# Down projections of two feed-forward layers by seven block products instead of eight

## The chip, the cores and the metric

The kernel runs on one core of a Trainium2 chip. Times are device microseconds, for one launch of the whole kernel. Five engines with instruction queues of their own work beside each other: TensorE (PE; the load of its stationary operand is listed as PEld), VectorE (DVE), ScalarE (ACT), GpSimd (POOL) and SyncE (SP), which issues the DMAs. Each works its queue strictly in order, so an instruction that waits holds up all that stand behind it there.

## The reference

One decoder layer over 512 tokens of width 1024, all in float32. Each feed-forward layer is a SwiGLU with 2816 inner columns, added at half weight:

```
x = x + 0.5 * swiglu(rms_norm(x, ffn1_norm), w_gate, w_up, w_down)
...        # attention and RWKV-7 mixing, projected in by w_in and out by w_out, added to x
x = x + 0.5 * swiglu(rms_norm(x, ffn2_norm), w_gate, w_up, w_down)

def swiglu(h, w_gate, w_up, w_down):
    return (jax.nn.silu(h @ w_gate) * (h @ w_up)) @ w_down
```

The down projection is the last product: 512 x 2816 by 2816 x 1024.

## The kernel before

A float32 product is made of three matmuls on rounded parts (`mm3`, lines 71 to 77): each operand is split into a high part, by a cast on ScalarE, and a rest, by a subtraction on VectorE, and high x high, high x rest and rest x high are summed in PSUM. Weights come in tiles of 512 KB. `weights` (lines 62 to 70) issues the load into one of three raw buffers (`raw_...`, line 64), casts it (`hi_...`, line 68) and subtracts (`lo_...`, line 69); of each of the two results there are two buffers.

*Gate and up* (`ffn`) take 22 blocks `f` of 128 inner columns. For each, two weight tiles (gate, up) meet the transposed input (`xa` in layer 1, `xc` in layer 2) in 2 x 8 x 3 matmuls of 128x512; SiLU (line 197) and a product (line 198) give `sg`, 128 inner columns by 512 tokens, which is split into `hh` and `hl` (lines 205, 206), the stationary operands of down. For the first block, the token columns come in two halves, and the norms and transposes of the last two token tiles are called in between (`proj_into` with `hook`).

*Down* (`rows_out`, lines 149 to 185) takes the 1024 output columns in two halves. In each, 11 groups of two blocks (one weight tile a group) are multiplied into four PSUM accumulators, one for each tile of 128 tokens. The last four groups are held back and finished tile by tile, so that a tile's addition into x (line 173), its norm (`norm_T`) and its transposes run under the next tile's matmuls. What comes after the last tile is handed to the next product as `hook`.

The order of instructions on an engine is that of the program as a list scheduler has merged it; it follows data, buffers and a few fixed pairs (`keep_in_program_order`). A tile that is allocated waits until the last user of its buffer is done.

Of the kernel before, what the change touches and what calls it, by code (L numbers as in the profile page):

```python
# [42 lines left out]
def tile_layer(ctx: ExitStack, tc: tile.TileContext, I, out):  # L43
# [99 lines left out]
    def rows_out(wsrc, n_grp, lhs, resid, scale, ptile, extra, done, name, dump=None, store=None, begun=None):  # L143
# [41 lines left out]

    def ffn(n, xT, x, hpool, ptile, extra, hook, done, w0, store):
        hT = []
# [31 lines left out]
    with ExitStack() as c:  # L219
        xpool = c.enter_context(tc.tile_pool(name="x1", bufs=1, reuse_waits="tile"))  # L220
        hpool = c.enter_context(tc.tile_pool(name="h1", bufs=1, reuse_waits="tile"))
        extra = c.enter_context(tc.tile_pool(name="e1", bufs=2, reuse_waits="tile"))
# [55 lines left out]
    with ExitStack() as c:  # L278
        xpool = c.enter_context(tc.tile_pool(name="x2", bufs=1, reuse_waits="tile"))
        xcpool = c.enter_context(tc.tile_pool(name="xc", bufs=4, reuse_waits="tile"))  # L280
        hpool = c.enter_context(tc.tile_pool(name="h2", bufs=1, reuse_waits="tile"))
# [776 lines left out]
```

## Time and profile before

| | us |
|---|---|
| median of 3 runs | 1140.79 |
| lowest, highest of the runs | 1138.6, 1566.35 |
| profiled execution, its own time | 1137.05 |
| its span, first to last instruction | 1135.3 |
| TensorE busy, share of the span | 1103.2, 97% |
| VectorE, ScalarE, GpSimd busy | 494.4, 383.9, 139.2 |
| DMA, mean over the span | 111.88 MB, 99 GB/s |

All numbers of the profile are of one execution, whose span lies between its first and last instruction. The first layer's gate and up run from about 18 to 257 us, its down to 379, mixing to about 770, the second layer's gate and up to about 1011 and its down to 1131. Matmuls are pipelined, so the duration of one contains a part of the next; the distance of their starts tells the pace.

### The profile page before, as it was taken

The page shows a single profiled execution, that of the slowest core. Times are in us where ns is not written, and L with a number is a line of the kernel's source. Part 1 is how long each engine was busy: PE and PEld are TensorE (multiplying, and loading weights), DVE is VectorE, ACT ScalarE, POOL GpSimd, SP SyncE. Part 2 cuts the span into 40 slices and gives each one's busy share as a digit, 9 for nine tenths or more (in the row PEclk, how much of TensorE's full clock was granted, in tenths as well). Part 3 has the DMA queues.
Part 4 walks back from the last instruction along what each step waited for, and adds up shares of the span by engine and source line. Part 5 has one row for each costly group of instructions (what it writes and reads, how often), then busy time and mean ns, then how long its engine had stood idle before and what let it go on. Part 6 is the DMA issues. An engine that isn't in the chain of part 4 may idle for free.

```text
span 1135.3 us, 13758 instructions
## 1 busy us (share of the span) xinstructions
PE 1103.2 (97%) x5512; PEld 921.3 (81%) x5512; DVE 494.4 (44%) x815; ACT 383.9 (34%) x604; POOL 139.2 (12%) x185
## 2 busy tenths in 40 slices
PE   7999999999999999998899999999999999999998
PEld 6888888888888977777788898779888888888887
DVE  5333333332223545695478467644333333332222
ACT  4322233222222356524343534433322232222120
POOL 3000000000000346302432211212000000000000
PEclk9999999999999999998899999999999999999999
DMA  5322332223224424542321200422223322233321
GB/s 189 111 93 96 105 97 93 93 100 105 93 93 148 163 69 102 150 130 83 94 63 60 90 23 29 148 75 94 93 93 103 101 93 93 95 105 104 122 94 56
DMA packets 53202, 111.88 MB, mean 99 GB/s; under 512 B 20721, under 2 KB 26097, under 8 KB 53138
## 3 DMA queue, kind: packets, MB, share of 16 engines
q1 hardware_dynamic: 53138, 111.00, 30.2%
q8 instruction: 43, 0.70, 0.3%
q14 instruction: 21, 0.17, 0.0%
HBM read 100.50 MB, written 9.44 MB: 97 GB/s over the span
## 4 chain that ended last, share of the span: by engine, by line
PE 85%; DVE 7%; ACT 3%; POOL 2%; issue 2%; DMA 1%; SPq 0%; POOLq 0%; ACTq 0%; DVEq 0%
PE gu L77 14%; PE gu L73 14%; PE gu L76 14%; PE accd L76 7%; PE accd L73 7%; PE accd L77 7%; PE in L77 3%; PE in L76 3%; PE in L73 3%; PE aa L844 1%; PE cx L870 1%; PE po L768 1%; PE cn L887 1%; DVE pr L642 1%; PE acco L76 1%
## 5 line engine op out<-in xcount | busy, mean ns | idle before, releaser
L68 ACT CAST hi_gu<-raw_gu 128x1024 fp32r<-128x1024 f32 x88 | 92.7, 1054 | 316.9 <-PE gu L76 299.6
L69 DVE TENSOR_TENSOR lo_gu<-raw_gu,hi_gu 128x1024 fp32r<-128x1024 f32 x84 | 102.9, 1225 | 158.5 <-ACT hi_gu L68 154.6
L76 PE MATMUL accd<-lo_d,hh 128*128 128x512 f32 x288 | 112.3, 390 | 0.0
L77 PE MATMUL accd<-hi_d,hl 128*128 128x512 f32 x288 | 112.1, 389 | 0.0
L73 PE MATMUL accd<-hi_d,hh 128*128 128x512 f32 x288 | 112.0, 390 | 0.0
L69 DVE TENSOR_TENSOR lo_d<-raw_d,hi_d 128x1024 fp32r<-128x1024 f32 x44 | 53.3, 1224 | 127.4 <-ACT hi_d L68 127.0
L68 ACT CAST hi_d<-raw_d 128x1024 fp32r<-128x1024 f32 x44 | 45.6, 1052 | 152.7 <-PE accd L77 133.0
L198 DVE TENSOR_TENSOR sg<-gu,sg 128x512 f32<-128x512 f32 x44 | 30.4, 692 | 143.2 <-PE gu L77 141.8
L76 PE MATMUL gu<-xa0l,hi_gu 128*128 128x512 f32 (+1 forms) x184 | 70.0, 380 | 0.5 <-DVE xa0l L130 0.5
L73 PE MATMUL gu<-xa0h,hi_gu 128*128 128x512 f32 (+1 forms) x184 | 70.1, 381 | 0.3 <-ACT xa0h L129 0.3
L73 PE MATMUL gu<-xc0h,hi_gu 128*128 128x512 f32 (+1 forms) x184 | 70.0, 380 | 0.0
L73 PE MATMUL gu<-xc1h,hi_gu 128*128 128x512 f32 (+1 forms) x184 | 70.0, 380 | 0.0
L73 PE MATMUL gu<-xa1h,hi_gu 128*128 128x512 f32 (+1 forms) x184 | 70.0, 380 | 0.0
L76 PE MATMUL gu<-xc0l,hi_gu 128*128 128x512 f32 (+1 forms) x184 | 69.9, 380 | 0.0
L77 PE MATMUL gu<-xc0h,lo_gu 128*128 128x512 f32 (+1 forms) x184 | 69.9, 380 | 0.0
L76 PE MATMUL gu<-xa1l,hi_gu 128*128 128x512 f32 (+1 forms) x184 | 69.9, 380 | 0.0
L76 PE MATMUL gu<-xc1l,hi_gu 128*128 128x512 f32 (+1 forms) x184 | 69.9, 380 | 0.0
L77 PE MATMUL gu<-xc1h,lo_gu 128*128 128x512 f32 (+1 forms) x184 | 69.9, 380 | 0.0
L77 PE MATMUL gu<-xa0h,lo_gu 128*128 128x512 f32 (+1 forms) x184 | 69.9, 380 | 0.0
L77 PE MATMUL gu<-xa1h,lo_gu 128*128 128x512 f32 (+1 forms) x184 | 69.9, 380 | 0.0
L76 PEld LDWEIGHTS accd<-lo_d,hh 128*128 128x128 f32 x288 | 54.1, 188 | 11.6 <-DVE lo_d L69 0.5
L73 PEld LDWEIGHTS accd<-hi_d,hh 128*128 128x128 f32 x288 | 53.9, 188 | 11.5 <-ACT hi_d L68 0.4
(349 smaller groups left out, 2253.4 us busy)
## 6 DMA issues: line engine op xcount, KB each, us to landing
raw_gu<-in_ffn_w_gu SPq DMA_DIRECT2D x88, 512.0 KB, 3.4
raw_d<-in_ffn_w_down SPq DMA_DIRECT2D x44, 512.0 KB, 3.4
raw_in<-in_w_in SPq DMA_DIRECT2D x28, 512.0 KB, 3.9
raw_o<-in_w_out SPq DMA_DIRECT2D x8, 512.0 KB, 3.4
x<-in_x SPq DMA_DIRECT2D x4, 512.0 KB, 5.8
xd<-x SPq DMA_DIRECT2D x4, 512.0 KB, 2.6
xr<-ard SPq DMA_DIRECT2D x8, 256.0 KB, 4.5
bk<-bkd SPq DMA_DIRECT2D x4, 512.0 KB, 4.3
```

The source lines that it names most:

```text
L68: A.copy(out=hi, in_=raw)
L69: (lo_eng or V).tensor_tensor(out=lo, in0=raw, in1=hi.bitcast(F32), op=ALU.subtract)
L73: first = T.matmul(ps, lh, rh, start=start, stop=False)
L76: T.matmul(ps, lh, rl, start=False, stop=False)
L77: T.matmul(ps, ll, rh, start=False, stop=stop)
L198: V.tensor_tensor(out=sg, in0=ps[1], in1=sg, op=ALU.mult)
L642: V.tensor_tensor(out=pr[:, :n1, :n2], in0=au[:, i + 1:, i:i + 1].broadcast_to([P, n1, n2]), in1=tu[:, i:i + 1, :n2].broadcast_to([P, n1, ...
L768: T.matmul(po[:, h, 0:65], pw[:, j * P:(j + 1) * P], va[:, j, h, 0:65], start=(j == 0), stop=(j == qi))
L844: T.matmul(ps[:, c], bk[:, j, c], xr[:, j, c, 2 * h:2 * h + 2], start=True, stop=True)
L870: T.matmul(px[:, j, h], xr[:, j, c, 2 * h:2 * h + 2].rearrange("p a b -> p (a b)"), sv[:, j, h, c, :], start=True, stop=True)
L887: T.matmul(pn[:, j, h], kr[:, j, c, 2 * h:2 * h + 2].rearrange("p a b -> p (a b)"), sv[:, j, h, c, :], start=True, stop=True)
```

## The change

Strassen's scheme multiplies 2x2 blocks with seven products instead of eight. The blocks are here: for activations, token half (tiles 0, 1 and 2, 3) by even or odd block `f` of a pair; for weights, even or odd `f` by column half. Four of the seven products take a sum of weight blocks and one more takes two weights' sums: five sums (128x512 each) for each of the 11 pairs. `sums_ahead` loads both halves of a pair's weights during gate and up, makes the sums on VectorE, and stores them in DRAM (`sd`: three, `s17`: two). `combine` makes the sums of activations from two `sg`. `down` then runs three stages of 11 groups: products 3 and 5, products 1 and 7, products 4, 2 and 6, whose last three groups are held back. Each product has two accumulators, for the two tiles of a token half, and is added into one or two places of x by `add`. Between stages, `split` turns the activation buffers into the next stage's sums. The down projection of mixing (`w_out`) still uses `rows_out`.

A layer's down issues 66 weight loads where it had 22: in the first stage and in the third, a tile comes as two loads of 256 KB.

```diff
-    def ffn(n, xT, x, hpool, ptile, extra, hook, done, w0, store):
-        hT = []
...
+    def sums_ahead(n):
+        wd = I[f'ffn{n}_w_down']
+        sd = dpool.tile([NG, 3, P, S], F32, name=f"sd{n}")
+        s17 = dpool.tile([NG, P, D], F32, name=f"s17{n}")
+        def steps():
+            t = ra = rb = None
+            for g in range(NG + 1):
+                if g:
+                    for o, i in ((sd[g - 1, 0:2].rearrange("j p s -> p j s"), t), (sd[g - 1, 2], rb[:, 0]), (s17[g - 1], ra)):
+                        tc.keep_in_program_order(Q.dma_start(out=o, in_=i.rearrange("p a b -> p (a b)") if i is ra else i))
+                if g == NG:
+                    return
+                ra, rb = (npool.tile([P, 2, S], F32, tag="xn", name=f"r{k}{n}_{g}") for k in "ab")
+                for k, z in enumerate((ra, rb)):
+                    tc.keep_in_program_order(Q.dma_start(out=z.rearrange("p a b -> p (a b)"), in_=wd[k, g]))
+                yield
+                t = npool.tile([P, 2, S], F32, tag="gain", bufs=1, name=f"s{n}_{g}")
+                V.tensor_tensor(out=t[:, 0], in0=rb[:, 0], in1=rb[:, 1], op=ALU.subtract)
+                V.tensor_tensor(out=t[:, 1], in0=ra[:, 1], in1=ra[:, 0], op=ALU.subtract)
+                V.tensor_tensor(out=rb[:, 0], in0=rb[:, 0], in1=ra[:, 0], op=ALU.add)
+                for j in range(2):
+                    V.tensor_tensor(out=ra[:, j], in0=ra[:, j], in1=rb[:, 1], op=ALU.add)
+                yield
+        return sd, s17, steps()
+    def combine(n, g, e, o, u, v, l):
+        V.tensor_tensor(out=u[0][:, 0], in0=e[:, 0:H], in1=o[:, H:S], op=ALU.add)
+        V.tensor_tensor(out=u[0][:, 1], in0=o[:, 0:H], in1=o[:, H:S], op=ALU.subtract)
+        V.tensor_tensor(out=u[1][:, 0], in0=e[:, H:S], in1=o[:, H:S], op=ALU.add)
+        V.tensor_tensor(out=u[2], in0=e[:, H:S], in1=e[:, 0:H], op=ALU.subtract)
+        A.copy(out=u[1][:, 1], in_=o[:, H:S])
+        split(v[:, 0], l[:, 0], e[:, 0:H])
+        V.tensor_tensor(out=o[:, 0:H], in0=e[:, 0:H], in1=o[:, 0:H], op=ALU.add)
...
+    def split(hi, lo, src):
+        A.copy(out=hi, in_=src)
+        V.tensor_tensor(out=lo, in0=src, in1=hi.bitcast(F32), op=ALU.subtract)
+    def down(n, U, VV, LL, x, ptile, xp, extra, sd, s17, done, dump, store):
+        wd = I[f'ffn{n}_w_down']
+        cnt = [0]
+        def loaded(name, *src, keep=None, to=None):
+            raw = wpool.tile([P, 2, S], F32, tag="wraw", bufs=3, name=f"raw_{name}")
...
+                for j, z in enumerate(src):
+                    Q.dma_start(out=raw[:, j], in_=z)
+            if to:
+                hi, lo = to
+                for j in range(len(hi)):
+                    A.copy(out=hi[j], in_=raw[:, j])
+                    V.tensor_tensor(out=lo[j], in0=raw[:, j], in1=hi[j].bitcast(F32), op=ALU.subtract)
+                return
+            cnt[0] += 1
...
+            A.copy(out=hi, in_=raw)
+            V.tensor_tensor(out=lo, in0=raw, in1=hi.bitcast(F32), op=ALU.subtract)
+            return hi, lo
...
+        def prod(acc, g, hl, w, ts=(0, 1), last=NG - 1):
+            for t in ts:
+                lh, ll = (z[:, t * P:(t + 1) * P] for z in hl)
+                mm3(acc[t], lh, ll, w[0], w[1], g == 0, g == last)
...
+        def add(acc, t, r, c, sign):
+            tt = 2 * r + t
+            xs = x[tt][:, c * S:(c + 1) * S]
+            V.scalar_tensor_tensor(out=xs, in0=acc[t], scalar=0.5 * sign, in1=xs, op0=ALU.mult, op1=ALU.add)
+            if (tt, c) in final and store:
...
+        def both(ma, mb, g, v, l, hi, lo):
+            pend.append((g, v, l, hi, lo))
+            if g != NG - 2:
+                for j, m in enumerate((ma, mb)):
+                    for g_, v, l, hi, lo in pend:
+                        prod(m, g_, (v[:, j], l[:, j]), (hi[:, j], lo[:, j]))
+                pend.clear()
...
+        for g in range(NG):
+            v, l = VV[g], LL[g]
+            hi, lo = loaded(f"d1{n}_{g}", sd[g, 0], wd[1, g][:, S:D])
+            both(m3, m5, g, v, l, hi, lo)
+            for k in (g - 1, g) if g == NG - 1 else (g,) if g != NG - 2 else ():
+                split(VV[k], LL[k], U[k][0])
+        for t in range(2):
+            add(m3, t, 0, 1, 1)
+            add(m3, t, 1, 1, 1)
+        for t in range(2):
+            final.add((t, 1))
+            add(m5, t, 0, 1, 1)
+            add(m5, t, 0, 0, -1)
+        ms = [None] * NT
...
+        def turn(g):
+            split(VV[g], LL[g], U[g][1])
+            if g == 0:
...
+                x6.append(VV[g - 4])
+            split(x6[g][:, 0], x6[g][:, 1], U[g][2])
+        m1, m7 = accs(1), accs(7, "tp")
+        for g in range(NG):
+            v, l = VV[g], LL[g]
+            hi, lo = loaded(f"d2{n}_{g}", s17[g])
+            both(m1, m7, g, v, l, hi, lo)
+            if g >= NG - 3:
+                turn(g - NG + 3)
...
+        m4, m2, m6 = accs(4), accs(2), accs(6)
+        keep = 3
+        held, w6 = [], {}
+        for g in range(NG):
+            v, l = VV[g], LL[g]
+            kept = g >= NG - keep
+            hi, lo = loaded(f"d3{n}_{g}", wd[0, g][:, 0:S], sd[g, 1],
...
+            if g % 2 == 0:
+                gs = [k for k in (g, g + 1) if k < NG]
+                if g < NG - keep:
+                    h6, l6 = loaded(f"d6{n}_{g}", *(sd[k, 2] for k in gs))
...
+                else:
+                    for k in gs:
+                        w6[k] = tuple(LL[2 * (k - NG + keep) + p].rearrange("p a b -> p (a b)") for p in range(2))
+                    loaded(f"d6{n}_{g}", *(sd[k, 2] for k in gs), to=([w6[k][0] for k in gs], [w6[k][1] for k in gs]))
+            z = ((v[:, 1], l[:, 1]), (hi[:, 1], lo[:, 1])), ((v[:, 0], l[:, 0]), (hi[:, 0], lo[:, 0])), ((x6[g][:, 0], x6[g][:, 1]), w6[g])
+            if kept:
+                held.append((g, z))
+            else:
+                for m, (a_, w) in zip((m4, m2, m6), z):
+                    prod(m, g, a_, w)
+            if g + 3 < NG:
+                turn(g + 3)
+        def finish(i, m, t):
+            for g, z in held:
+                prod(m, g, *z[i], ts=(t,))
...
+        for t in range(2):
+            finish(0, m4, t)
+            add(m4, t, 0, 0, 1)
+            nxt[t] = done(t, ms[t])
...
+        for t in range(2):
+            add(m4, t, 1, 0, 1)
+        for t in range(2):
+            finish(1, m2, t)
+            final.add((2 + t, 0))
+            add(m2, t, 1, 0, 1)
+            add(m2, t, 1, 1, -1)
...
+            if nxt[t]:
+                nxt[t]()
...
+        for t in range(2):
+            finish(2, m6, t)
+            final.add((2 + t, 1))
+            add(m6, t, 1, 1, 1)
+            nxt[2 + t] = done(2 + t, ms[2 + t])
+        return nxt[2:]
...
+        sd, s17, ahead = sums_ahead(n)
...
+            sg = hpool.tile([P, S], F32, tag="sg", bufs=3 if n == 1 else 2, name=f"sg{n}_{f}")
...
+            if f % 2 == 0:
+                e = sg
             else:
...
-            A.copy(out=hi, in_=sg)
-            V.tensor_tensor(out=lo, in0=sg, in1=hi.bitcast(F32), op=ALU.subtract)
-            hT.append((hi, lo))
-        return rows_out(I[f'ffn{n}_w_down'], NG, lambda f, tt: tuple(h[:, tt * P:(tt + 1) * P] for h in hT[f]),
...
+                combine(n, g, e, sg, u, v, l)
...
+            if f >= 1:
+                next(ahead, None)
+            if f == NF - 1:
+                for _ in range(3):
+                    next(ahead, None)
+        return down(n, U, VV, LL, x, ptile, xp, extra, sd, s17, done,
+                    n == 1 and (lambda: hpool.tile([P, S], F32, tag="sg", bufs=3, name="dump")), store)
```

**How instructions move.** VectorE at the start of layer 1. In the rows `xa0l` and `xa1l` are the rests of the transposed input, `lo_gu1_1_0` that of the gate weights of block 1; the number at a name's end is a buffer's. Before:

```order
L130 TENSOR_TENSOR xa0l_99<-pTa20_229,xa0h_98 128x4x128
L130 TENSOR_TENSOR xa1l_101<-pTa21_236,xa1h_100 128x4x128
L130 TENSOR_TENSOR xa0l_99<-pTa30_255,xa0h_98 128x4x128
L130 TENSOR_TENSOR xa1l_101<-pTa31_262,xa1h_100 128x4x128
L69 TENSOR_TENSOR lo_gu1_1_0_339<-raw_gu1_1_0_336,hi_gu1_1_0_338 128x1024
L198 TENSOR_TENSOR sg1_0_329<-gu1_0_1_204,sg1_0_329 128x512
```

Now, where `s1_0`, `ra1_0` and `rb1_0` are the first pair's sums and loaded blocks:

```order
L131 TENSOR_TENSOR xa0l_99<-pTa20_231,xa0h_98 128x4x128
L131 TENSOR_TENSOR xa1l_101<-pTa21_238,xa1h_100 128x4x128
L131 TENSOR_TENSOR xa0l_99<-pTa30_257,xa0h_98 128x4x128
L212 TENSOR_TENSOR s1_0_481<-ra1_0_412 128x512
L131 TENSOR_TENSOR xa1l_101<-pTa31_264,xa1h_100 128x4x128
L211 TENSOR_TENSOR s1_0_481<-rb1_0_413 128x512
L215 TENSOR_TENSOR ra1_0_412<-ra1_0_412,rb1_0_413 128x512
L213 TENSOR_TENSOR rb1_0_413<-rb1_0_413,ra1_0_412 128x512
L215 TENSOR_TENSOR ra1_0_412<-ra1_0_412,rb1_0_413 128x512
L69 TENSOR_TENSOR lo_gu1_1_0_337<-raw_gu1_1_0_334,hi_gu1_1_0_336 128x1024
```

The first sum stands ahead of `xa1l` of the last token tile, and the other four ahead of the weights of block 1. The block that the first sum reads is loaded into a buffer of tile 2's norm.

VectorE at the end of layer 1's down. Before, with `lo_d11k` the weights of group k of the second half:

```order
L69 TENSOR_TENSOR lo_d117_2360<-raw_d117_2357,hi_d117_2359 128x1024
L69 TENSOR_TENSOR lo_d119_2372<-raw_d119_2369,hi_d119_2371 128x1024
L69 TENSOR_TENSOR lo_d118_2366<-raw_d118_2363,hi_d118_2365 128x1024
L69 TENSOR_TENSOR lo_d1110_2378<-raw_d1110_2375,hi_d1110_2377 128x1024
L173 SCALAR_TENSOR_TENSOR x1_0_94<-accd110_2143,x1_0_94 128x512
L117 SCALAR_TENSOR_TENSOR xnb0_2413<-x1_0_94,rsb0_2416,gain_mix_norm_2406 128x512 x2
L173 SCALAR_TENSOR_TENSOR x1_1_95<-accd111_2144,x1_1_95 128x512
```

Now, with `d31_k` the tile for products 4 and 2 of group k, `d61_k` that for product 6, `v1_k` activations:

```order
L259 TENSOR_TENSOR lo_d31_8_2712<-raw_d31_8_2708,hi_d31_8_2711 128x1024
L249 TENSOR_TENSOR l1_1_553<-raw_d61_8_2715,l1_0_400 128x512
L232 TENSOR_TENSOR v1_5_1176<-u1_9_1802,v1_5_1176 128x256
L249 TENSOR_TENSOR l1_3_865<-raw_d61_8_2715,l1_2_709 128x512
L259 TENSOR_TENSOR lo_d31_7_2683<-raw_d31_7_2679,hi_d31_7_2682 128x1024
L232 TENSOR_TENSOR v1_6_1332<-u1_10_1958,v1_6_1332 128x256
L259 TENSOR_TENSOR lo_d31_9_2726<-raw_d31_9_2722,hi_d31_9_2725 128x1024
L249 TENSOR_TENSOR l1_5_1177<-raw_d61_10_2736,l1_4_1021 128x512
L259 TENSOR_TENSOR lo_d31_10_2733<-raw_d31_10_2729,hi_d31_10_2732 128x1024
L275 SCALAR_TENSOR_TENSOR x1_0_94<-m4_10_2448,x1_0_94 128x512
L275 SCALAR_TENSOR_TENSOR x1_2_96<-m4_10_2448,x1_2_96 128x512
```

Group 8's tiles and a split of activations stand ahead of `lo_d31_7`, whose raw buffer `raw_d31_9` waits for; the first additions of product 4 come behind `lo_d31_10`.

GpSimd at the end of layer 1: `rsb` is the factor of a tile's norm, `lo_in6` the weights of the next projection. Before:

```order
L114 TENSOR_SCALAR rsb1_2450<-ssb11_2448,msd11_2081 128x1
L115 TENSOR_TENSOR rsb1_2450<-rsb1_2450,nhalf_73 128x1
L114 TENSOR_SCALAR rsb2_2498<-ssb21_2496,msd12_2111 128x1
L115 TENSOR_TENSOR rsb2_2498<-rsb2_2498,nhalf_73 128x1
L69 TENSOR_TENSOR lo_in6_0_2612<-raw_in6_0_2609,hi_in6_0_2611 128x1024
L69 TENSOR_TENSOR lo_in6_1_2618<-raw_in6_1_2615,hi_in6_1_2617 128x1024
```

Now (the rows left out are eight fills of one column each):

```order
L115 TENSOR_SCALAR rsb1_2779<-ssb10_2777,msd11_2230 128x1
L116 TENSOR_TENSOR rsb1_2779<-rsb1_2779,nhalf_73 128x1
L101 TENSOR_SCALAR msd12_2800<-ssd120_2798 128x1
L69 TENSOR_TENSOR lo_in6_0_2931<-raw_in6_0_2928,hi_in6_0_2930 128x1024
L69 TENSOR_TENSOR lo_in6_1_2937<-raw_in6_1_2934,hi_in6_1_2936 128x1024
L101 TENSOR_SCALAR msd13_2830<-ssd130_2828 128x1
...
L115 TENSOR_SCALAR rsb2_2860<-ssb21_2858,msd12_2800 128x1
L116 TENSOR_TENSOR rsb2_2860<-rsb2_2860,nhalf_73 128x1
L115 TENSOR_SCALAR rsb3_2879<-ssb31_2877,msd13_2830 128x1
L116 TENSOR_TENSOR rsb3_2879<-rsb3_2879,nhalf_73 128x1
```

`rsb2` was ahead of both `lo_in6`, with only `rsb3` behind them; now both stand behind.

## Rows read from the trace of the kernel before

**Rows 1.** The page: busy time and share by engine, then the chain by engine.
```profile
PE 1103.2 (97%) x5512; PEld 921.3 (81%) x5512; DVE 494.4 (44%) x815; ACT 383.9 (34%) x604; POOL 139.2 (12%) x185
...
PE 85%; DVE 7%; ACT 3%; POOL 2%; issue 2%; DMA 1%; SPq 0%; POOLq 0%; ACTq 0%; DVEq 0%
```

**Rows 2.** Stretches (from:to, length, busy us by engine, granted clock, DMA share, GB/s).
```profile
22.00:140.00 118.00, 118.00 (x548) 98.76 (x547) 41.72 (x45) 36.29 (x45) 0.00 (x0) 1.00 0.28 94
...
257.00:378.00 121.00, 121.00 (x542) 99.75 (x541) 38.32 (x40) 30.98 (x42) 5.34 (x11) 1.00 0.31 105
...
790.00:1010.00 220.00, 220.00 (x972) 182.19 (x971) 75.60 (x81) 63.72 (x80) 0.00 (x0) 1.00 0.29 97
...
1012.00:1131.00 119.00, 119.00 (x525) 97.90 (x524) 31.30 (x30) 21.82 (x22) 0.00 (x0) 1.00 0.28 95
```

**Rows 3.** TensorE in time (start, us): first accd matmul of layer 1, the 25th.
```profile
256.72 0.39 PE L73 MATMUL accd<-hi_d,hh 128*128 128x512 f32 x1
...
262.16 0.39 PE L73 MATMUL accd<-hi_d,hh 128*128 128x512 f32 x1
```

**Rows 4.** Groups by line: operation, shape, count, busy us, mean ns, idle before.
```profile
L69 DVE TENSOR_TENSOR lo_gu<-raw_gu,hi_gu 128x1024 fp32r<-128x1024 f32 x84 | 102.9, 1225 | 158.5 <-ACT hi_gu L68 154.6
...
L69 DVE TENSOR_TENSOR lo_d<-raw_d,hi_d 128x1024 fp32r<-128x1024 f32 x44 | 53.3, 1224 | 127.4 <-ACT hi_d L68 127.0
...
L68 ACT CAST hi_d<-raw_d 128x1024 fp32r<-128x1024 f32 x44 | 45.6, 1052 | 152.7 <-PE accd L77 133.0 <-PE gu L76 15.4 <-issue 4.0
...
L198 DVE TENSOR_TENSOR sg<-gu,sg 128x512 f32<-128x512 f32 x44 | 30.4, 692 | 143.2 <-PE gu L77 141.8 <-ACT sg L197 1.4
...
L206 DVE TENSOR_TENSOR hl<-sg,hh 128x512 fp32r<-128x512 f32 x36 | 24.6, 685 | 0.0
...
L173 DVE SCALAR_TENSOR_TENSOR x<-accd,x 128x512 f32<-128x512 f32 x16 | 11.1, 692 | 47.3 <-PE accd L77 47.3
...
L847 DVE TENSOR_TENSOR kr<-aa,cst 128x256 f32<-128x256 f32 x16 | 6.6, 415 | 0.2
```

**Rows 5.** Stretches, as in the second group: the start of mixing's input projection.
```profile
380.00:390.00 10.00, 9.98 (x84) 9.75 (x83) 3.90 (x6) 2.75 (x6) 4.99 (x13) 1.00 0.93 315
```

**Rows 6.** DMA issues (KB, median us to landing); last, down weight loads of 1085 to 1116.
```profile
raw_d<-in_ffn_w_down SPq DMA_DIRECT2D x44, 512.0 KB, 3.4
...
x<-xd SPq DMA_DIRECT2D x4, 512.0 KB, 6.7
...
out_y<-x SPq DMA_DIRECT2D x8, 256.0 KB, 2.0
...
DMA to landing us min/median/max: 3.4/3.5/4.5
```

**Rows 7.** TensorE in time, layer 1's start: tile 2's transposes; first use of xa1l, tile 3.
```profile
17.45 1.29 PE L124 MATMUL pTa<-ident,xna 128*128 128x128 f32 x8 [1.62 <-DVE xna L117]
...
24.01 0.28 PE L76 MATMUL gu<-xa1l,hi_gu 128*128 128x256 f32 x1
```

**Rows 8.** Layer 1's end in time: POOL, VectorE, and TensorE's last row.
```profile
375.86 5.29 POOL L69 TENSOR_TENSOR lo_in<-raw_in,hi_in 128x1024 fp32r<-128x1024 f32 x2 [0.78 <-DVE xnb L117]
...
381.35 0.28 POOL L114 TENSOR_SCALAR rsb<-ssb,msd 128x1 f32<-128x1 f32 x1
...
378.77 0.69 DVE L173 SCALAR_TENSOR_TENSOR x<-accd,x 128x512 f32<-128x512 f32 x1 [1.64 <-PE accd L77]
...
382.30 1.42 DVE L117 SCALAR_TENSOR_TENSOR xnb<-x,rsb,gain_mix_norm 128x512 f32<-128x512 f32 x2 [1.78 <-POOL rsb L115]
...
383.76 1.27 PE L124 MATMUL pTb<-ident,xnb 128*128 128x128 f32 x8
```

**Rows 9.** VectorE in time: the last addition of the kernel.
```profile
1131.72 0.69 DVE L173 SCALAR_TENSOR_TENSOR x<-accd,x 128x512 f32<-128x512 f32 x1 [4.75 <-PE accd L77]
```

**Rows 10.** Stretches in mixing, as in the second group.
```profile
510.00:520.00 10.00, 6.44 (x27) 4.66 (x25) 9.62 (x17) 4.68 (x12) 3.97 (x7) 1.00 0.16 54
...
520.00:530.00 10.00, 9.58 (x41) 8.45 (x42) 3.03 (x6) 4.63 (x12) 2.24 (x4) 0.66 0.07 26
```

More of the change, by code (lines that the diff above doesn't have):

```diff
@@ L184, in rows_out @@
         return [late]
[L186 to L187 removed]
+    H = S // 2
+    def sums_ahead(n):
[22 more added lines that the diff above has]
+        return sd, s17, steps()
@@ new lines, in combine @@
+    def combine(n, g, e, o, u, v, l):
[6 more added lines that the diff above has]
+        V.tensor_tensor(out=o[:, 0:H], in0=e[:, 0:H], in1=o[:, 0:H], op=ALU.add)
+        split(v[:, 1], l[:, 1], o[:, 0:H])
@@ L188, in ffn @@
+    def ffn(n, xT, x, hpool, ptile, xp, extra, hook, done, w0, store):
+        U, VV, LL, big = [], [], [], []
+        sd, s17, ahead = sums_ahead(n)
         for f in range(NF):
@@ L205, in ffn @@
-            A.copy(out=hi, in_=sg)
-            V.tensor_tensor(out=lo, in0=sg, in1=hi.bitcast(F32), op=ALU.subtract)
-            hT.append((hi, lo))
-        return rows_out(I[f'ffn{n}_w_down'], NG, lambda f, tt: tuple(h[:, tt * P:(tt + 1) * P] for h in hT[f]),
-                        x, 0.5, ptile, extra, done, f"d{n}", n == 1 and (lambda: hpool.tile([P, S], F32, tag="sg", bufs=2, name="dump")), store)
+            if f % 2 == 0:
+                e = sg
+            else:
+                g = f // 2
+                v, l = (hpool.tile([P, 2, H], F32R, tag=t, bufs=NG, name=f"{t}{n}_{g}") for t in "vl")
+                if n == 2 and g in (4, 5):
+                    ua, ub = big[2 * g - 8:2 * g - 6]
+                    u = ua[:, 5:7], ub[:, 5:7], ua[:, 7]
+                else:
+                    if n == 2 and g < 4:
+                        z = tpool.tile([P, 8, H], F32, tag="xT", name=f"u{n}_{g}")
+                        big.append(z)
+                    else:
+                        z = hpool.tile([P, 5, H], F32, tag="u", bufs=NG if n == 1 else NG - 6, name=f"u{n}_{g}")
+                    u = z[:, 0:2], z[:, 2:4], z[:, 4]
+                combine(n, g, e, sg, u, v, l)
+                U.append(u)
+                VV.append(v)
+                LL.append(l)
@@ L225, in tile_layer @@
         xT = new_xT("xa")
-        one = hpool.tile([1, P], F32, name="one")
+        one = spool.tile([1, P], F32, tag="ao", bufs=2, name="one")
         G.memset(one, 1.0)
@@ L301, in tile_layer @@
         pc.close()
+        ec.close()
         ptile = psum_tiles(c, 3)
         w0 = [weights(I['ffn2_w_gu'][0, gu], P, f"gu2_0_{gu}", lo_eng=G) for gu in range(2)]
-        ffn(2, state['xT'], x2, hpool, ptile, extra, hook,
+        hpool = c.enter_context(tc.tile_pool(name="h2", bufs=1, reuse_waits="tile"))
+        ffn(2, state['xT'], x2, hpool, ptile, xcpool, None, hook,
             lambda tt, ms: None, w0, out)
```

56 lines of the change are left out of this document (44 added, 12 removed).

## The prediction, made before the changed kernel ran

> **What bounds the kernel now.** I read the page's busy shares and its chain first [rows 1]: TensorE is busy 97% of the span and 85% of the chain of waits runs on it, while VectorE is busy 44%. A share over the whole span hides the stages, so next I took the table by stretches [rows 2]: in gate and up of both layers and in both down stages TensorE is busy for the whole of each stretch at a granted clock of 1.00 (the upper level, 2.4 GHz), and VectorE for about a third or less (41.7 of 118 us in the first gate and up, 38.3 of 121 in its down). So here a matmul less is time less, as long as the other engines keep up.
>
> The price of a matmul is its spacing, not its duration. In the order of time of TensorE's instructions the first `accd` matmul starts at 256.72 and the 25th at 262.16 [rows 3]: 5.44 / 24 = 0.2267 us (the groups' means of 0.39 include the overlap of neighbours).
>
> **The change part by part.** Before, a layer's down takes 2 halves x 11 groups x 2 x 4 tiles x 3 = 528 matmuls of 128x512; now 11 x 7 products x 2 tiles x 3 = 462 of the same shape. 66 less in each of two layers is 132 x 0.2267 = **29.9 us off**. The rest is what stands against it.
>
> *Gate and up, steady state: 0.* For a pair of f blocks TensorE has 96 matmuls, 21.76 us. VectorE had 4 `lo_gu` of 1.225, 2 `sg` and 2 `hl` of 0.69 [rows 4]: 7.6 us. It loses the two `hl` and gets five sums of 128x512 (0.685 each, from `hl`) and seven operations of 128x256 (0.415, from `kr`): 12.6 us of 21.76. ScalarE gives up two casts for three of half the width. Bytes: 2.1 MB a pair before; two reads of 512 KB and writes of 512, 256 and 512 KB come to it, 4.46 MB in 21.76 us, 205 GB/s. The stretch 380 to 390 shows 315 GB/s [rows 5]. SP now waits, with loads of `raw_gu` queued behind, for the sums that it stores and then for these stores, before it may fetch the next blocks (landing 2.0 to 3.4 us, [rows 6]). A load that comes some 3 us later still arrives, since three raw buffers are in flight and a weight tile lasts 5.4 us. If this cover were gone, each of 22 pairs could lose up to about 1 us; both ends go into the range.
>
> *Start of gate and up: 1.4 (0 to 6).* On VectorE the first sum, `s1_0`, now stands ahead of the second half's `xa1l` of tile 3, and the sums ahead of `lo_gu1_1_0`. The blocks' load goes into a buffer that tile 2's transposes free, at 18.7 us [rows 7]. A landing of 3.4 after an issue of 0.3 gives 22.4; two operations of 0.69 end at 23.8, and TensorE takes the tile at 24.01 [rows 7]: nothing lost. At the 6.7 that four such loads in a row took [rows 6] it would be 27.1, 3.1 lost. I take 0.7 at each layer's start, nearer to the usual landing.
>
> *Supply in the down stages: 0 in steady state.* A 512 KB weight tile fed 24 matmuls (5.44 us); now 12 (2.72 us), 193 GB/s where the stretch of before shows 105 [rows 2]. Its raw buffer is one of three, so a turn may take 8.16 us. It takes two issues of 0.33, a landing of 3.4 to 4.5 [rows 6], a cast of 1.05 and a subtraction of 1.22 [rows 4]: 6.3 to 7.4. That holds by 0.8 to 1.9 us. This is the thinnest cover of the change. VectorE itself has, in the third stage, 1.5 tiles x 1.22 and about 1.1 of splits for a group of 18 matmuls (4.08 us): 2.9, it keeps up.
>
> On landing, rows show 3.4 for 512 KB and 2.0 for a 256 KB store. The Trainium skill (DMA: Bandwidth & Descriptors, Anatomy of one DMA) has a fixed 2.0 us and 1 us for 436 KB, measured for transfers issued by GpSimd; as an estimate that gives 3.2 and 2.6. By it a tile in two halves would be there sooner than I take it, and the loss at the kept groups below would be about 1.2 a layer, not 2.2.
>
> *First to second stage: 1.2 (0 to 4).* Eight additions of 0.69 into x come in a burst, and `lo_d2_2` must wait for stage one's last matmul before its buffer is free. Four additions and the subtraction, 4.0 us, stand against 24 matmuls, 5.4, that are ready. I take 0.6 a layer for the splits in the same queue.
>
> *Kept groups: 4.4 (0 to 10.4).* Three groups are held back and finished tile by tile, 9 matmuls (2.04 us) each. `raw_d3_9` can be fetched only when `lo_d3_7` has freed its raw buffer. From there: issue and landing 4.1 to 5.2, cast 1.05, subtraction 1.22: 6.3 to 7.4, then `lo_d3_10`, 7.5 to 8.7. TensorE wants `lo_d3_9` 5.0 and `lo_d3_10` 5.7 us after `lo_d3_7`, if that came just in time: 1.8 to 3.0 lost; up to 2 us of lead take nearly all of it away. VectorE's queue also has the conversions of group 8 ahead of `lo_d3_7`; with these late the loss is 5.2. I take 2.2 a layer.
>
> *End of layer 1: 2.2 (0 to 5).* Two tiles' norms are now left over instead of one. Before, the last addition is at 378.77 and that tile's transposes at 383.76 [rows 8], 5.0 us covered by the next projection. Now tile 2's transposes come after 24 half-width matmuls (2.9 us) and tile 3's last nine (2.0). On POOL `rsb2` now stands behind `lo_in6_0` and `lo_in6_1`, which took 5.29 together [rows 8] and wait for buffers that the kept groups free. From these 4.1 us before the last matmul, cast 1.05, 5.3, the norm and its scaling 2.4 (381.35 to 383.72, [rows 8]) end at +4.6; the transposes want it at +2.9: 1.7, and I round up for the additions between.
>
> The end of the kernel keeps its shape: last matmul, one addition of 0.69 [rows 9], one store.
>
> Sum: -29.9 + 1.4 + 1.2 + 4.4 + 2.2 = **-20.7**. The profiled execution took 1137.05 us (span 1135.3), so 1116.4. It lies 3.7 below the median of 1140.79; with the run of 1138.6 the three lie around 1138.6, so I add 1.6: **1118 us**.
>
> **The rivals.**
>
> *All covers hold* (loads land at 3.4, conversions run ahead): only 2 or 3 us are lost, 1138.6 - 27 to 1138.6 - 29.9: 1109 to 1112. For it speaks that TensorE never waits in the 578 us of [rows 2]; against it, the kept groups, where the arithmetic leaves under 2 us.
>
> *The ring of three raw buffers becomes the bound*, and the kernel gets slower. With three buffers the time per tile is a third of the turn. At a landing of 6.7, as the four loads `x<-xd` in a row had [rows 6], a turn is 0.66 + 6.7 + 2.27 = 9.6, 3.21 a tile; over 2 x 38 tiles 0.49 x 76 = 37 more, 7 more than the matmuls give: 1146. It decides from a turn of 9.3 (2.72 + 29.9 / 76 = 3.11 a tile), a landing of 6.4. Against it: 4.5 is the longest landing among the down loads in the rows, and three tiles in flight ask for 193 GB/s of a measured 315. At 8 us it would be 40 slower, past the bound below.
>
> *The clock falls.* Between 510 and 520 TensorE is busy 6.4 of 10 us, and in the ten after that the granted clock is 0.66, a mix of the two levels, at 9.6 busy [rows 10]. Such a stretch costs 3.4 us. The gaps that I expect are of 1 to 3 us in ten; if all five bigger ones draw a fall, 15 more: 1133.
>
> *Each transfer pays its own price.* The change cuts a tile's load into two of 256 KB in stages one and three. At 2.0 for each of 55 halves and 3.4 for 11 wholes [rows 6], one after another, a layer's down would take 147 us of transfers against 462 x 0.2267 = 105 of matmuls: 42 more a layer, 1138.6 + 84 - 30 = 1193. The rows speak against it: 315 GB/s is two loads of 512 KB in 3.4 us, so transfers overlap. The Trainium skill (DMA: Bandwidth & Descriptors, Bandwidth) has the rule that stands behind this case, to batch into 1 MiB or more.
>
> **How the numbers follow.** Chances: the forecast 0.56, all covers hold 0.20, the clock 0.12, the ring 0.09, serial transfers 0.03. A measurement of this kernel can tell about 2%, 22.8 us of 1140.8, from no change; that bound lies at 1118, right at the forecast, so its cases split: somewhat under half go to faster (losses under 7 of an expected 9.2), with all of the second case: 0.25 + 0.20 = 0.45. Slower by 2% are the serial case and some of the ring's: 0.05. Within 2%: 0.50. The range takes in the clock and leaves out the ring and the serial transfers: 1108 to 1134. The forecast's own range is 1112 to 1127.
>
> **What would show it.** TensorE's count down by 132. Gate and up busy throughout at clock 1.00, with VectorE near 69 of 118 us and about 200 GB/s. In the down stages idle time before `m1`, `m4` and the `in` matmuls, released by VectorE's `lo_d`, and none in the middle of a stage. A DMA landing of `raw_d` over 6 us, or ScalarE's `hi_d` waiting for DMA at every tile, would prove the ring right; a granted clock under 1 in a down stage, the clock; idle time all through gate and up would mean that SP's waits reach TensorE, which I priced at nothing.

## The result and the profile after

The changed kernel takes 1111.5 us (median of four runs, 1104.35 to 1115.87) against 1140.8: 0.9735 of the time before, 95% interval 0.9697 to 0.9774, about 30 us less. The 1140.8 is the median of three runs of before; a fourth took 1566.35, far from all others, and is left out. The forecast was 1118, 20.7 less by its own sum. The profiled execution is the slowest of the four, 1115.87 with a span of 1114.1, only 21.2 below the span of before. So before any cause there is a question of size: 21 by the spans, 26 if the 5.3 are taken out by which mixing is longer in the changed kernel's trace (below), or 30 by the medians?

The page after, busy time and then the chain by engine, answers to [rows 1]:

```profile
PE 1080.0 (97%) x5380; PEld 903.9 (81%) x5380; DVE 677.9 (61%) x1169; ACT 449.2 (40%) x728; POOL 140.0 (13%) x185
...
PE 78%; DVE 9%; DMA 4%; POOL 3%; ACT 3%; issue 3%; SPq 0%; ACTq 0%; POOLq 0%; DVEq 0%
```

5512 matmuls have become 5380, 132 fewer. The chain now has 4% of DMA. The stretches of the feed-forward layers, for [rows 2]:

```profile
22.00:140.00 118.00, 118.00 (x551) 98.92 (x550) 64.59 (x99) 36.41 (x51) 0.00 (x0) 1.00 0.59 200
...
256.00:370.00 114.00, 112.53 (x517) 92.93 (x516) 86.01 (x113) 63.51 (x96) 10.78 (x23) 1.00 0.63 203
...
790.00:1000.00 210.00, 210.00 (x928) 173.91 (x927) 113.07 (x174) 61.20 (x87) 0.00 (x0) 1.00 0.63 212
1000.00:1112.00 112.00, 110.22 (x485) 90.60 (x484) 80.85 (x103) 56.35 (x76) 0.00 (x0) 1.00 0.56 184
```

Gate and up: TensorE without a gap at 200 to 212 GB/s, VectorE 64.6 of 118 (near 69 expected). In the down stages VectorE is at three quarters. What TensorE waited for there, from 250 to 380 us and then from 760 to 1000 (us in all, times, longest):

```profile
PE pTb L125 <- DVE xb0l L131: 1.6, 2, 1.3
PE m L76 <- DVE lo_d L259: 0.2, 1, 0.2
```

```profile
PE gu L76 <- DVE xc0l L131: 1.0, 1, 1.0
```

With 0.2 more before `m` in layer 2 these are 3.0 us, where 9.2 were forecast. The rest of the difference between the spans lies where the change touches nothing. For each kernel the stages, bounded by first matmuls (gate and up until 0.45 us after the start of its last one; the first expectations below drew that line 0.2 earlier):

| us | gate, up 1 | down 1 | mixing | gate, up 2 | down 2 | mean clock |
|---|---|---|---|---|---|---|
| before | 245.0 | 122.4 | 391.1 | 241.2 | 119.6 | 0.988 |
| before, again | 245.0 | 122.4 | 399.5 | 241.2 | 119.6 | 0.979 |
| changed | 244.7 | 108.5 | 396.4 | 242.5 | 104.7 | 0.980 |
| changed, again | 245.0 | 108.5 | 395.4 | 242.7 | 104.5 | 0.983 |
| changed, third | 245.1 | 109.3 | 392.8 | 242.5 | 105.6 | 0.985 |
| layer 1 alone | 244.9 | 108.4 | 386.2 | 241.2 | 119.6 | 0.994 |
| mended | 244.9 | 108.1 | 397.2 | 241.3 | 105.2 | 0.979 |
| mended, again | 245.2 | 108.7 | 391.2 | 241.2 | 104.9 | 0.988 |
| no sums | 244.7 | 110.0 | 396.8 | 241.2 | 106.2 | 0.980 |
| whole loads | 245.1 | 111.0 | 391.8 | 242.5 | 105.2 | 0.988 |
| two raw buffers | 245.1 | 133.4 | 400.1 | 251.2 | 118.9 | 0.972 |

The four feed-forward stages of before return to 0.1 us (728.2), those of the change within 2.1 (700.4, 700.7, 702.5; in the third the kept groups wait 0.8 in each down). They are 25.7 to 27.8 below before. Mixing, which the change leaves alone, runs from 386 to 400, broadly in step with the clock.

### The profile page after: what moved, and what is told of

It is laid out like the page before. It is cut to its first block, busy times and chain, and to the rows that moved or that the text cites. A ratio compares the mean times of both kernels' runs of the same rounds, so it can differ in the third digit from the quotient of the medians.

```text
span 1114.1 us, 14426 instructions
## 1 busy us (share of the span) xinstructions
PE 1080.0 (97%) x5380; PEld 903.9 (81%) x5380; DVE 677.9 (61%) x1169; ACT 449.2 (40%) x728; POOL 140.0 (13%) x185
## 4 chain that ended last, share of the span: by engine, by line
PE 78%; DVE 9%; DMA 4%; POOL 3%; ACT 3%; issue 3%; SPq 0%; ACTq 0%; POOLq 0%; DVEq 0%
PE gu L76 14%; PE gu L77 14%; PE gu L73 14%; PE m L76 4%; PE m L77 4%; PE m L73 4%; PE in L76 3%; PE in L77 3%; PE in L73 3%; DMA raw_d<-sd 3%; PE aa L1069 1%; PE cx L1095 1%; PE cn L1112 1%; PE po L993 1%; DVE pr L867 1%
## 5 line engine op out<-in xcount | busy, mean ns | idle before, releaser
L259 DVE TENSOR_TENSOR lo_d<-raw_d,hi_d 128x1024 fp32r<-128x1024 f32 x39 | 47.5, 1223 | 18.4 <-ACT hi_d L258 18.2
L76 PE MATMUL m<-lo_d,v 128*128 128x512 f32 x148 | 57.9, 391 | 0.4 <-DVE lo_d L259 0.4
L73 PE MATMUL m<-hi_d,v 128*128 128x512 f32 x148 | 57.7, 390 | 0.0
L259 DVE TENSOR_TENSOR w_d<-raw_d,w_d 128x1024 fp32r<-128x1024 f32 x35 | 42.7, 1222 | 21.0 <-ACT w_d L258 21.0
L77 PE MATMUL m<-hi_d,l 128*128 128x512 f32 x140 | 54.5, 389 | 0.0
L73 PE MATMUL in<-xb0h,hi_in 128*128 128x512 f32 (+1 forms) x120 | 50.0, 417 | 2.9 <-ACT kts L933 2.9
L76 PE MATMUL m<-w_d,v 128*128 128x512 f32 x132 | 51.4, 389 | 0.0
```

The costliest lines, as they stand in the source:

```text
L73: first = T.matmul(ps, lh, rh, start=start, stop=False)
L76: T.matmul(ps, lh, rl, start=False, stop=False)
L77: T.matmul(ps, ll, rh, start=False, stop=stop)
L259: V.tensor_tensor(out=lo, in0=raw, in1=hi.bitcast(F32), op=ALU.subtract)
```

## The experiments

**Is the change 21, 26 or 30 us?** Both kernels once more, unedited.

> The changed kernel once more. Stages counted by first matmuls (gate and up 1, down 1, mixing, gate and up 2, down 2); the first trace had 244.4, 108.8, 396.4, 242.2, 105.0 us, before had 244.7, 122.7, 391.1, 240.9, 119.9. Theory: the feed-forward stages are the same from execution to execution, so 244.4, 108.8, 242.2, 105.0 return within 0.5 each, 26 us below before in sum; mixing is untouched and its length follows the granted clock, anywhere from 386 to 397, which is why the time scatters by 10 us and the first trace showed only 21 less. Rival: the change itself made mixing 5 us longer, then mixing is 396 again within 1; or shorter (the mean of the four times, 29 below before), then it is 388 within 1. Ratio to before 0.973 by the theory with an interval of some 0.004.

> The kernel before once more, for a second trace. Theory: 244.7, 122.7, 240.9, 119.9 return within 0.5 each, and mixing differs from 391.1 by some us in step with its granted clock. Rival: mixing is 391 within 1, so that the 396.4 of the changed kernel was its own.

Measured: 1112.6 against 1138.9, ratio 0.9777 (0.9745 to 0.9808); before against itself 1.0014. The two traces of before differ by 8.4 us in mixing and by nothing elsewhere. The stretches from 680 to 720 us: before, then before again, then changed:

```profile
680.00:700.00 20.00, 19.21 (x133) 17.52 (x132) 16.82 (x44) 9.88 (x20) 2.98 (x5) 0.94 0.14 41
700.00:720.00 20.00, 18.49 (x129) 16.48 (x129) 15.74 (x50) 9.97 (x22) 3.53 (x5) 0.98 0.00 1
```

```profile
680.00:700.00 20.00, 19.21 (x133) 17.14 (x132) 16.64 (x46) 9.76 (x19) 2.83 (x4) 0.99 0.14 40
700.00:720.00 20.00, 19.14 (x84) 18.10 (x84) 10.70 (x36) 7.61 (x19) 3.10 (x3) 0.50 0.00 1
```

```profile
680.00:700.00 20.00, 18.35 (x92) 16.90 (x90) 12.10 (x39) 6.36 (x16) 2.03 (x3) 0.62 0.00 1
700.00:720.00 20.00, 18.09 (x108) 16.12 (x108) 13.42 (x34) 7.89 (x18) 4.32 (x4) 0.87 0.16 45
```

In one execution the granted clock (third column from the right) holds, in another it stands at 0.50, the lower level of 1.2 GHz, for 20 us, with 84 matmuls where 129 fit. The first rival had mixing at 396 again within 1, and the second trace of the change does have 395.4, so that trace alone would not refute it. What does: before itself drew 399.5, a third trace of the change 392.8, and the mean clock is 0.985 over 50 runs of before as over 15 of the change. The 396 was drawn, not caused. (The expectation's sum was off: its own four stages make 27.8 less, not 26.)

This gives a sharper measure than the ratio. Over all runs here, fitted together, the time falls on lines of one slope, 0.81 us for each 0.001 of mean granted clock, with 1.06 us left over (a straight line for each kernel, 50 runs of before, 15 of the change; these two alone give 0.86 and the same difference). At equal clock the change is **27.2 us faster, plus or minus 0.6**. The 30 of the first four runs and the 21 of the spans are both draws of mixing's clock. A third run of the change, for which I expected 27.4 at equal clock and a mean clock of 0.986, gave 26.8 and 0.984.

**One part alone.** Layer 2 went back to its old functions and pools:

```diff
-        ffn(2, state['xT'], x2, hpool, ptile, xcpool, None, hook,
+        ffn_old(2, state['xT'], x2, hpool, ptile, extra, hook,
```

> Layer 1 by seven products, layer 2 as before. Theory: down 1 108.8 us, gate and up 2 and down 2 as before (240.9, 119.9): 13.9 less than before in the stages, ratio 0.988 with the scatter of mixing. Rival (mixing gains by what layer 1 hands it): 17 or more less, ratio 0.985 or below. A third, that half of the gain belongs to each layer by the matmuls alone: 15.0 less.

Measured: ratio 0.9899 (0.9867 to 0.9930); at equal clock 14.0 less, plus or minus 0.9; down 1 14.0 shorter, layer 2 to the tenth as before. This is the theory's 13.9; the third value, 15.0, lies just outside. For layer 2 it leaves 13.2 of the 27.2, and its stages have 13.6 (14.9 less in down, 1.3 more in gate and up): the layers add up.

**Do the sums beside gate and up cost anything?** The calls of `next(ahead, None)` went, and down loaded plain blocks (so its result is another one):

```diff
-            if f >= 1:
-                next(ahead, None)
...
-            hi, lo = loaded(f"d2{n}_{g}", s17[g])
+            hi, lo = loaded(f"d2{n}_{g}", wd[0, g])
```

> The changed kernel without the sums of weight blocks: nothing is loaded, summed or stored for them in gate and up, and down loads plain weight blocks of the same size in their place. Theory: loads, sums and stores beside gate and up cost nothing but the wait at layer 2's start: gate and up 1 244.9, gate and up 2 241.2 (242.6 with them), down 1 and 2 as with them within 0.4. Rival: the doubled DMA traffic or SP's waits cost TensorE some tenths per pair of blocks, then both gate and ups are shorter by 2 us or more; or reading back what was just stored is slower, then the downs are shorter by 1 or more.

Gate and up 1 is the same (244.7), gate and up 2 1.3 shorter, just the wait at its start. Half of the 4.46 MB a pair, the five sums and SP's waits for stores thus cost nothing in steady state. The two runs, 1114.9 and 1117.7, are at equal clock 2.1 slower (plus or minus 1.6) than the change, not faster. The downs became longer rather than shorter, by 1.5 to 1.7 against the first two traces of the change and 0.6 to 0.7 against the third, with waits of 0.8 and 0.4 in the kept groups and 1.3 in layer 2. Whether plain blocks come later than stored sums, or this is the spread of the kept groups, was not settled.

**Do halves cost more than whole tiles?**

```diff
-                for j, z in enumerate(src):
-                    Q.dma_start(out=raw[:, j], in_=z)
+                if len(src) == 2:
+                    Q.dma_start(out=raw.rearrange("p a b -> p (a b)"), in_=s17[whole.pop()])
```

> The changed kernel with every tile of the first and third stage of down loaded whole, by one DMA of 512 KB from the stored sums of products 1 and 7 (so those products get other data). Theory: halves cost nothing, since transfers overlap and the ring holds: down 1 108.5 and down 2 104.6, each within 0.4, and at most the 0.4 before product 4's kept groups goes. Rival (the skill's rule on small transfers, each half paying its own fixed cost): down 1 and 2 shorter by 1 us or more, landings at least 1 us earlier for a tile.

Down 1 111.0, down 2 105.2: no gain. Two waits of 1.7 and 0.5 at the start of down 1 are the edit's own: its first tiles read the pairs stored last, and ScalarE waited for them. Landings of this kernel's tiles, and the same issues of the changed kernel:

```profile
raw_d<-s SPq DMA_DIRECT2D x76, 512.0 KB, 4.2
```

```profile
raw_d<-sd SPq DMA_DIRECT2D x66, 256.0 KB, 3.5
...
raw_d<-in_ffn_w_down SPq DMA_DIRECT2D x44, 256.0 KB, 3.4
raw_d<-s SPq DMA_DIRECT2D x22, 512.0 KB, 4.2
```

A second half issued 0.3 to 0.4 us later is there no later than a whole. The rule of the Trainium skill (DMA: Bandwidth & Descriptors, Bandwidth) is to batch into 1 MiB or more; no run here loads 1 MiB at once, but the step towards it, from 256 to 512 KB, gains nothing with three tiles in flight.

**Does the ring of three raw buffers decide?** Two attempts to take one buffer away by placeholders left all three in use, since a placeholder gave its buffer back at once; those runs repeat the changed kernel (1111.9 and 1111.6). The third holds one until product 4's first addition:

```diff
+        pin = wpool.tile([P, 2, S], F32, tag="wraw", bufs=3, name=f"pin{n}")
+        G.memset(pin[:, 0, 0:1], 0.0)
...
             add(m4, t, 0, 0, 1)
+            if t == 0:
+                G.tensor_tensor(out=spool.tile([P, 1], F32, tag="pin", bufs=1, name=f"unpin{n}"), in0=pin[:, 0, 0:1],
+                                in1=x[0][:, 0:1], op=ALU.add)
```

> The changed kernel in whose down stages one of the three raw buffers is held by a placeholder until product 4's first addition, so that the 39 loads of a layer share two (in both earlier attempts the placeholders gave their buffer back at once, and all three went on carrying weights: those two runs were the changed kernel over again). Theory (supply holds by the ring of three): from the traces a turn is one or two issues 0.3 to 0.8, landing 3.5 to 4.2, cast 1.05, subtraction 1.22, 6.1 to 7.3, so with two buffers a tile every 3.05 to 3.6 us where TensorE takes 2.72 (2.64 in the third stage): 39 times 0.3 to 0.9, down 1 122 to 142 us instead of 108.5 to 109.3, down 2 118 to 138 instead of 104.4 to 105.6; gate and up unchanged. Rival (the conversions run so far ahead of TensorE that the ring never decides): both below 112.

Measured: 1167.2 against 1143.8 of before beside it, ratio 1.0208 (1.0162 to 1.0255): the change with two buffers is slower than before, and 44 us slower than with three at equal clock (55 as measured). SyncE in time, four tiles of the first stage:

```profile
271.27 0.33 SPq L246 DMA_DIRECT2D raw_d<-sd  x1
271.64 0.43 SPq L246 DMA_DIRECT2D raw_d<-in_ffn_w_down  x1
274.22 0.33 SPq L246 DMA_DIRECT2D raw_d<-sd  x1
...
277.00 0.33 SPq L246 DMA_DIRECT2D raw_d<-sd  x1
...
279.87 0.33 SPq L246 DMA_DIRECT2D raw_d<-sd  x1
```

ScalarE there, each cast after a wait for its load:

```profile
271.88 1.05 ACT L260 CAST w_d<-raw_d 128x1024 fp32r<-128x1024 f32 x1 [1.38 <-DMA raw_d<-in_ffn_w_down]
...
274.67 1.05 ACT L260 CAST hi_d<-raw_d 128x1024 fp32r<-128x1024 f32 x1 [1.21 <-DMA raw_d<-in_ffn_w_down]
```

A tile every 2.86 us, a buffer's turn 5.73 (271.27 to 277.00): loads land sooner when two are in flight (median 2.9 to 3.1 for a half), so here it is below the 6.1 to 7.3 that I expected. Over all 39 tiles of the layer the issues lie 3.03 us apart (257.30 to 372.44), just under the 3.05 to 3.6. TensorE, from 245 to 405 us, waits 8.3 us for weights, where the change with three buffers waits 0.2 to 0.8, and the layer's end holds back norms:

```profile
PE pTb L125 <- DVE xb0l L131: 5.1, 1, 5.1
PE m L76 <- DVE w_d L261: 3.5, 3, 2.2
PE m L73 <- ACT hi_d L260: 2.5, 3, 1.3
PE in L73 <- DVE x L277: 2.1, 1, 2.1
PE m L76 <- DVE lo_d L261: 1.4, 3, 0.8
PE m L73 <- ACT w_d L260: 0.9, 3, 0.4
```

So the ring decides, but not all of the 44 us is its waits. Gate and up 2, which I expected unchanged, takes 8.7 longer with TensorE busy throughout. Its stretch beside one of the same length of the changed kernel above (790 to 1000, 928 matmuls):

```profile
820.00:1030.00 210.00, 210.00 (x901) 168.91 (x900) 110.50 (x170) 59.50 (x84) 0.10 (x1) 1.00 0.60 200
```

27 matmuls are missing at a granted clock of 1.00 and without a gap: they start 0.233 us apart instead of 0.227, as most do in this trace's feed-forward stages from down 1's first wait on (in mixing's projection between them the pace is 0.227), and in no other trace here. That is some 6 of the 8.7; a fall of the clock (0.91 from 800 to 820 us) and a longer wait at the start (1.8 for 1.0) make up the rest. What slows the matmuls is not known. The clock also falls beside the waits: from 320 to 330 us TensorE is busy 8.2 of 10 us, and in the next ten the granted clock is 0.85, where the changed kernel holds 1.00.

**Can the remaining waits be taken out?** A first try moved the first sum behind the last transposed tile, and product 4's additions into tiles 2 and 3, with product 2's, behind the transposes (`issue_after` puts what it holds behind an instruction of the same engine):

```diff
+                with tc.issue_after(tr):
+                    V.tensor_tensor(out=t[:, 0], in0=rb[:, 0], in1=rb[:, 1], op=ALU.subtract)
...
-            add(m4, t, 1, 0, 1)
...
+            with tc.issue_after(state['e'][1].ins):
+                add(m4, t, 1, 0, 1)
```

> The changed kernel with two orders mended: the first sum on VectorE behind the last transposed tile, and product 4's additions into tiles 2 and 3 behind the transposes of tiles 0 and 1. Theory: TensorE's two longest waits in the feed-forward stages go (1.0 at the start of layer 2, 1.3 before tile 1's transposes): gate and up 2 241.2, down 1 107.5; 2.3 less than the changed kernel, 0.2% in the time, below what five rounds can tell. Rival: the additions are only moved, and tiles 2 and 3 are normed later, so 1 to 2 us appear in the first matmuls of mixing's projection.

The wait at layer 2's start went (241.2). Down 1 did not shrink: 109.0, still 1.6 before tile 1's transposes. 0.8 more, for tile 2's norm, falls into mixing's first matmuls, which is the rival's effect at a smaller size. Ratio 0.9808 (0.9776 to 0.9841), at equal clock 1.1 (plus or minus 1.1) slower than the change, with the four stages at 700.0 and that 0.8 outside them: no gain is shown. What I had blamed was wrong; VectorE of the changed kernel at layer 1's end shows the chain:

```profile
353.02 1.29 DVE L275 SCALAR_TENSOR_TENSOR x<-m,x 128x512 f32<-128x512 f32 x2 [0.83 <-PE m L77]
355.64 1.42 DVE L118 SCALAR_TENSOR_TENSOR xnb<-x,rsb,gain_mix_norm 128x512 f32<-128x512 f32 x2 [1.33 <-POOL rsb L116]
356.97 1.88 DVE L275 SCALAR_TENSOR_TENSOR x<-m,x 128x512 f32<-128x512 f32 x3
359.52 1.41 DVE L118 SCALAR_TENSOR_TENSOR xnb<-x,rsb,gain_mix_norm 128x512 f32<-128x512 f32 x2 [0.66 <-POOL rsb L116]
360.85 0.68 DVE L275 SCALAR_TENSOR_TENSOR x<-m,x 128x512 f32<-128x512 f32 x1
361.45 0.68 DVE L131 TENSOR_TENSOR xb0l<-pTb,xb0h 128x512 fp32r<-128x512 f32 x1
```

The addition into tile 1 (ready when TensorE leaves product 4 at 354.9) stands behind tile 0's norm, which waits 1.33 idle; so tile 1's norm is late, and tile 0's `xb0l`, whose PSUM buffer TensorE wants, stands behind that. The mended order breaks it at both places:

```diff
-            nxt[t] = done(t, ms[t])
+        for t in range(2):
+            with tc.issue_after(done_add[1, 0].ins):
+                nxt[t] = done(t, ms[t])
...
+            with tc.issue_after(e0):
+                add(m2, t, 1, 0, 1)
+                add(m2, t, 1, 1, -1)
```

> The changed kernel with the first sum behind the last transposed tile, and VectorE's order at layer 1's end mended where the trace of the last attempt shows the wait: product 4's addition into tile 1 ahead of tile 0's norm, the rests of tile 0's transposes ahead of product 2's additions. Theory (the 1.3 us before tile 1's transposes come from the chain addition, norm of tile 0, addition, norm of tile 1, rests of tile 0, in one queue): down 1 107.2 us where it was 108.5, gate and up 2 241.2 where it was 242.6, down 2 104.6; 2.7 less than the changed kernel at equal clock, 30 less than before. Rival: the later additions delay the norms of tiles 2 and 3, as they did in the last attempt (0.8), and down 1 stays at 108 to 109; then at equal clock 26 to 28 less than before.

> The mended order of VectorE once more, beside the changed kernel. In its first six runs it was 1.3 less at equal clock, yet its granted clock was 0.979 to 0.983 where the changed kernel had 0.980 to 0.994, so its median was no better. Theory (the clock in mixing is drawn anew in each execution, and six runs were a draw): its mean clock is within 0.002 of the changed kernel's now, and its median 1 to 2 us lower. Rival (the new order leaves mixing in another rhythm, in which the clock falls more): a mean clock of 0.982 or below again, 0.003 or more under the changed kernel's, and a median that is no lower.

The wait fell from 1.3 to 0.5 (mended kernel, again, 245 to 380 us):

```profile
PE m L76 <- DVE lo_d L263: 0.8, 1, 0.8
PE pTb L125 <- DVE xb0l L131: 0.5, 1, 0.5
```

Down 1 is 108.1 and 108.7, not 107.2: 0.5 of the wait stays, and the kept groups wait 0.6 to 0.8. That is the rival's length without its reason, since no wait for a norm of tiles 2 or 3 shows. In the second try it ran at 1110.1 beside 1113.2 of the changed kernel (ratios to before 0.9736 and 0.9760), 3.1 lower where 1 to 2 was expected. Over both tries and 12 runs it is 1.8 us (plus or minus 0.8) faster than the change at equal clock, 28.9 less than before, between the theory's 30 and the rival's 26 to 28. Its clock was 0.979 to 0.983 in the first six runs and 0.979 to 0.988 in the next, the changed kernel's 0.980 to 0.988 beside them (means 0.984 and 0.984): a draw, as the theory said. It is the fastest of these versions, by less than single runs can tell.

## Why the prediction was right, and where its sum was not

The direction, the mechanism and the range held; the time was 6.5 below the forecast, and just below the forecast's own range of 1112 to 1127. What came is the rival "all covers hold" (1109 to 1112, only 2 or 3 us lost), to which I gave 0.20 against 0.56. By the equal clock the gain is 27.2 where the sum had 20.7, so the losses were over-priced, 9.2 for 2.7.

*Matmuls, -29.9.* Right: 132 fewer, and 24 of them still take 5.44 us in the down of the change (342.82 to 348.26).

*Gate and up in steady state, 0.* Right, and shown by leaving the sums out. VectorE, the DMA share and SP's waits all grew as priced, and TensorE saw none of it.

*Start of gate and up, 1.4.* Near in size, a wait of 1.0 to 1.2 and a stage 1.3 to 1.5 longer, but nothing in layer 1 and all in layer 2. VectorE there waits for the first sum's blocks, and tile 3's rests stand behind it:

```profile
769.45 0.69 DVE L212 TENSOR_TENSOR s<-ra 128x512 f32<-128x512 f32 x1 [1.88 <-DMA ra<-in_ffn_w_down]
770.06 0.68 DVE L131 TENSOR_TENSOR xc0l<-pTc,xc0h 128x512 fp32r<-128x512 f32 x1
```

*Ring, 0.* Right that it holds. The margin was priced a little thin, 0.8 to 1.9 us of a turn of 8.16: by the changed kernel's own medians a turn that nothing else delays is 0.37 to the second issue, 3.4 to 3.5 landing, 1.05 and 1.22, so 6.0 to 6.1, an estimate that leaves 2.1. (The same sum with the landing of 3.1 gives the 5.7 of two buffers.) That one buffer fewer makes the change a loss was the slower rival's mechanism, by buffers instead of landings.

*First to second stage, 1.2.* Wrong in size: no wait is listed. The additions and the subtraction just fit into the ready work, and the splits did not push them out:

```profile
289.61 2.48 DVE L275 SCALAR_TENSOR_TENSOR x<-m,x 128x512 f32<-128x512 f32 x4
292.00 2.35 DVE L259 TENSOR_TENSOR lo_d<-raw_d,hi_d 128x1024 fp32r<-128x1024 f32 x2
```

The first of the two `lo_d` ends at about 293.2, and TensorE takes it at 293.27, a tenth late.

*Kept groups, 4.4.* This is the term that was mis-sized most: waits of 0.2 to 0.8 in layer 1, 0 to 0.8 in layer 2. The chain of waits of the changed kernel:

```profile
344.17 1.15 DVE lo_d L259
...
345.33 4.01 DMA raw_d<-sd
...
349.36 0.02 ACT l L248
...
349.89 1.06 ACT hi_d L258
...
350.97 1.24 DVE lo_d L259
...
352.25 0.50 PE m L76
```

The first `lo_d` is group 7's, the last group 10's. As forecast the chain starts where group 7 frees its raw buffer, but what is fetched into it is not group 9's tile (issued at 342.65) but product 6's last half, alone; the tile of group 10 was issued 1.1 us earlier (344.23) and waits only behind that half's cast (`l`) in ScalarE's queue. So group 10 is done 6.9 us after group 7, where 7.5 to 8.7 were priced, and TensorE wants it 5.4 after (5.7 priced). Just in time that would lose 1.5 a layer, not 1.8 to 3.0. The lead, which the prediction said would "take nearly all of it away" and then left out of the 2.2, is the rest. Group 7 is done at 345.30, and TensorE first takes it at 346.45:

```profile
344.08 1.22 DVE L259 TENSOR_TENSOR lo_d<-raw_d,hi_d 128x1024 fp32r<-128x1024 f32 x1
```

```profile
346.45 0.39 PE L76 MATMUL m<-lo_d,v 128*128 128x512 f32 x1
```

A lead of 1.15 us thus leaves 0.3 of the 1.5 (0.2 of it listed as a wait); in the other two traces of the change layer 1 has the same 6.9, leads of 0.95 and 0.25, and waits of 0.4 and 0.8.

*End of layer 1, 2.2.* Near in size, 1.6, wrong in place: not tiles 2 and 3 behind POOL's `lo_in6` but tile 1's transposes, by the order of VectorE.

*Scale.* The step from the profiled execution to the runs, +1.6, was smaller than the draw of mixing's clock, some 8 us between two executions of one kernel. With that, falls of the clock were there all along, in both kernels; the rival's own mechanism, falls from gaps of the change, does not show at gaps of 0.2 to 1.3 us, where the clock stays at 1.00 in the feed-forward stages. (Its price was also mis-added: five falls at 3.4 are 17, not 15, so 1135, past the range.)

## What to carry to other kernels

Where an engine is busy throughout a stage, removed work is gained nearly in full, here 27 of 30 us, as long as each load's turn (issue, landing, conversion) divided by its buffers stays below the work that a load feeds. A late chain costs its length less the time until its end is wanted, and less the lead with which it starts: price the lead too, from the trace. Before explaining the last third of a difference, compare stages: here those that the change touches return within 2.1 us while an untouched one moves by 14. When a wait names an instruction, read the queue ahead of it to the first idle time; the edit belongs there.

## What was not expected of the hardware

The mean granted clock of an execution varies with nothing changed, from 0.979 to 0.993 in 50 runs of before and from 0.980 to 0.994 in 15 of the change, and carries 0.81 us for each 0.001. With two raw buffers TensorE's pace in the feed-forward stages was 3% lower from its first wait on (0.233 us a matmul for 0.227), at a granted clock of 1.00, for a reason that no run here shows. Stores of 512 KB landed after 2.6 us in before (`xd`), and after 5.1 (`sd`) and 5.9 (`s17`) among the loads of gate and up, and no engine but SP is listed as waiting for them.
